# One table for the issue order of all five engines in a two-sublayer transformer step

## The chip, the cores and the metric

The kernel runs on one core of one Trainium2 chip. The metric is the device time of one execution in microseconds, as the median of several runs. The core has five engines that each issue their own instructions in a fixed sequence: TensorE (PE, with its weight loads as PEld), VectorE (DVE), ScalarE (ACT), GpSimd (POOL) and SyncE (SP), which issues most of the transfers (DMAs). An instruction waits on semaphores for what it needs from the other engines, and everything behind it on the same engine waits with it. So the same instructions in another order on an engine compute the same, and may end at another time.

## The reference

One encoder layer runs over 1024 prompt frames and over 64 sample frames, the latter with 512 cached rows. All of it is fp32.

```python
def in_proj(x, w_in, b_f):            # 1024 -> 3072 + 6 columns
    z = jnp.einsum('btd,de->bte', x, w_in)
    q_f, k_f, v_f, f_lg, u_g, v_g, q_s, k_s, v_s = jnp.split(z, _split_points(), axis=-1)
...
# FoX: softmax(q k / 8 + c_t - c_s) v, causal, c = cumsum(log_sigmoid(f))      6 heads x 64
# SB:  a = exp(log_sigmoid(z) + sum of log_sigmoid(-z) behind), a v, causal    6 heads x 64
# SGU: gelu(u) * (tril(W_s) LN(gelu(v)) + b), chunks of 128                    4 groups x 64
o = concat(o_fox, o_sgu, o_sb)
mix = (o * rsqrt(mean(o * o over a head) + RMS_EPS) * g_mix) @ w_out
x = layer_norm(ALPHA * x + mix, ln1_g, ln1_b)
x = layer_norm(ALPHA * x + square(relu(x @ w_up)) @ w_down, ln2_g, ln2_b)     # D_FF = 4096
```

The outputs are the two `x` and the new rows of keys, values, log forget gates and normalised gate values.

## The kernel before

Every fp32 operand of a large product is split into a high part (rounded to `fp32r`, by ACT) and the residue (by DVE or POOL, `lo_sub`, L98), and a product is three passes: high by high, high by low, low by high (`PASSES`). The MLP's products go by a scheme of seven block products in place of eight, with sums of weight blocks and of x blocks made beforehand.

The stages, by the times of the profile:

- **0 to about 560 us: projections and attention.** Chunks of x are loaded (`xr`, L312), transposed on PE (`xtp`, L321) and split into `xT`. Weights come as `raw` (L337) and are split (L338). Heads come in pairs: `kvfox`/`kvsb` (L362), `qfox`/`qsb` (L503), scores `Sfox`/`Ssb` (L561), softmax on ACT (`Tfox`, L536) or stick-breaking by ACT, a scan on DVE (`snsb`, L545) and a product on POOL (`sgsb`, L547). The probabilities are transposed into a PSUM tile `pt` (L609), split by ACT and DVE into `pth` (`split_pt`, L577 and L98), and multiplied with the values into `osb`/`ofox` (L619 to L622); the result is copied by ACT (`osbsb`/`osbfox`, L632) and transposed back (`otpsb`, L640). Gate projections `sgu` and `sgv` (L362) with their gelu (L758 to L761; `g1u4` and `g1u5` are those of chunks 4 and 5) and the gate's norm (L832 to L838) run beside it. `sgsb2s` and `snsb2s` belong to the sample frames.
- **The W_out steps** (`scale_wo`, L967 to L987) run beside the attention: sixteen times, a block of `w_out` is loaded into `rwo` (one buffer), scaled by `g_mix` and split into `swo` (one buffer) by ACT (L981) and DVE (L982), and stored to `wo_dr` in DRAM by two transfers (L985).
- **560 to 660 us: output projection** (`mx`, L251), with the heads' norm ahead of it (`sq`, L192, statistics `ss`, and `oTb`, L209).
- **660 to 730 us: the first layer norm**, x blocks `xo`, and the first up products.
- **730 to about 1040 us: the up product.** `Chain(p, s)` (product at L1294) makes the seven products of 256 columns `p` for a group `s` of rows, into four PSUM banks `zA` to `zD`. A bank is released by its reader: `sn` on ACT (L1305) for `zA`, sums on DVE (L1308, L1310) for others. `wr` are loaded weights (L1485), `wa` their splits (L1232), `ws` those of the sums (L1514).
- **About 1045 to 1385 us: the down product** (`Down`, L1756) from hidden rows that went through DRAM, with accumulators `acc` on DVE (L1721, L1723); then the last norms up to 1396 us.

What sets the order: the code is written as generators that are advanced in turn; the framework's scheduler then orders each engine's instructions by a simulated timeline and the dependencies. Some places take that freedom away: `in_order` gives each instruction that is traced inside it a dependency without a semaphore on the one traced before it on the same engine. `behind` does so with everything traced so far ahead of it. They stand around the W_out steps in the main loop (L1135), the first up chains (L1536, L1587, L1612 for PE alone, L1629), the last up chains (L1932) and the tail (L1999).

Of the kernel before, what the change touches and what calls it, by code (L numbers as in the profile page):

```python
# [2 lines left out]

# [1 line left out]

# [15 lines left out]
P = 128  # L21
PASSES = ((0, 0), (0, 1), (1, 0))
D = 1024
# [26 lines left out]
def build(tc, a):  # L50
    nc = tc.nc
    es = ExitStack()
    with es:
        _build(nc, tc, a, es)


def _build(nc, tc, a, es):
# [39 lines left out]
    def lo_sub(eng, out, src, hi):  # L97
        eng.tensor_tensor(out, src, hi.bitcast(F32), op=ALU.subtract)  # L98

    @contextmanager  # L100
    def in_order(prev=None, only=None):

        traced = nc.cur_bb.bb.instructions
        last = traced[-1]
        yield
        at = next(k for k in reversed(range(len(traced))) if traced[k] is last) + 1
        prev = {} if prev is None else prev
        for i in traced[at:]:
            if only is not None and i.engine != only:
                continue  # L110
# [179 lines left out]
    with ExitStack() as p1:  # L290
# [792 lines left out]
        F, A = fill(), attn()  # L1083
# [10 lines left out]
        while f_live or a_live:  # L1094
# [11 lines left out]
            if go_a:  # L1106
# [5 lines left out]
                try:  # L1112
                    c = next(A)
# [232 lines left out]
    for i in range(MIXED, NT):  # L1346
        t = ORD[i]
# [132 lines left out]
    with p3:  # L1480
# [148 lines left out]
        with in_order(border):  # L1629
# [20 lines left out]
            h4 = lp.tile([P, 2, 2, 2, 4, P], F32R, name="h4a", tag="ws")  # L1650
# [53 lines left out]
    with ExitStack() as p3:  # L1704
# [271 lines left out]
        c = NC - 1  # L1976
# [21 lines left out]
        g = 2 * c  # L1998
# [135 lines left out]
```

## Time and profile before

| | |
|---|---|
| median of 3 runs | 1400.99 us (1399.53 to 1404.98) |
| span of the profiled execution | 1396.1 us |
| median less span | 4.9 us |
| TensorE busy, idle in the span | 1324.3 us, 71.8 us |
| mean granted TensorE clock | 0.983 |
| HBM traffic over the span | 127 GB/s |

The profiled execution's time as a whole is not listed on its own; the span reaches from its first to its last instruction, and the median of the runs stands for the time around it. The page below cuts the span into 40 slices of 34.9 us; a digit is the busy share in tenths, and PEclk the clock that was granted to TensorE.

```profile
PE   7999999999988998999989999999998999999996
DVE  3576766676888288679866877777668677767677
ACT  4366665566656376334523322222256676667675
POOL 3222231245666355666422212212156765565557
PEclk9999999999999999999999999999999999999998
```

TensorE is near full in every slice but the first and the last; the other engines have free time in nearly all.

### The profile page before, as it was taken

Reading aid. Unit: us, or ns where it says so; the run is one execution under the profiler, and the core shown is the slowest. Engines: PE = TensorE matmul, PEld = TensorE weight load, DVE = VectorE, ACT = ScalarE, POOL = GpSimd, SP = SyncE. Lnnn points to the kernel's source line nnn. Section 1 sums busy time; section 2 is a strip of 40 time slices with the busy share of each in tenths; the row PEclk is TensorE's granted clock in tenths of the full one; section 3 lists DMA queues with packets and bytes.
Section 4 is the critical chain, followed back from the end, with each engine's and each line's share of the span. In section 5 each row is a group of like instructions: output and inputs, shape, how many; then the busy total and the mean of one; then the engine's idle time right before and its main releaser. Section 6 shows DMA issues by size and latency. Waiting matters only on the chain.

```text
span 1396.1 us, 24310 instructions
## 1 busy us (share of the span) xinstructions
PE 1324.3 (95%) x8827; PEld 1207.8 (87%) x8827; DVE 997.1 (71%) x1795; ACT 721.2 (52%) x1561; POOL 614.1 (44%) x667
## 2 busy tenths in 40 slices
PE   7999999999988998999989999999998999999996
PEld 7899989989987998778889999999986788887775
DVE  3576766676888288679866877777668677767677
ACT  4366665566656376334523322222256676667675
POOL 3222231245666355666422212212156765565557
PEclk9999999999999999999999999999999999999998
DMA  7355454231312346623234344443468344444343
GB/s 220 78 147 171 143 166 137 68 93 39 84 34 51 80 136 232 192 100 101 77 99 156 118 149 136 140 156 121 164 224 308 97 164 140 137 146 154 100 136 128
DMA packets 159088, 185.64 MB, mean 133 GB/s; under 512 B 27756, under 2 KB 117164, under 8 KB 158968
## 3 DMA queue, kind: packets, MB, share of 16 engines
q1 hardware_dynamic: 158968, 184.08, 41.8%
q8 instruction: 70, 1.15, 0.4%
q14 instruction: 50, 0.41, 0.1%
HBM read 117.65 MB, written 60.10 MB: 127 GB/s over the span
## 4 chain that ended last, share of the span: by engine, by line
PE 70%; DVE 10%; DMA 6%; ACT 5%; POOL 4%; issue 4%; SPq 1%; DVEq 0%; ACTq 0%; POOLq 0%
PE A L1756 9%; PE zA L1294 9%; PE zD L1294 6%; PE kvsb L362 5%; PE D L1756 5%; PE mx L251 5%; PE kvfox L362 4%; PE zB L1294 3%; PE zC L1294 3%; PE B L1756 2%; PE Sfox L561 2%; PE qfox L503 1%; PE qsb L503 1%; PE ptfox L609 1%; POOL wd L98 1%
## 5 line engine op out<-in xcount | busy, mean ns | idle before, releaser
L98 POOL TENSOR_TENSOR wa<-wr,wa 128x512 fp32r<-128x512 f32 x42 | 64.7, 1568 | 226.3 <-ACT wa L1232 226.3
L98 POOL TENSOR_TENSOR wd<-rd,wd 128x512 fp32r<-128x512 f32 x77 | 100.6, 1318 | 108.0 <-ACT wd L1232 99.3
L251 PE MATMUL mx<-xT,oTb 128*128 128x512 f32 (+1 forms) x416 | 105.2, 404 | 1.5 <-DVE oTb L98 1.5
L1294 PE MATMUL zA<-xo,ws 128*128 128x288 f32 (+1 forms) x720 | 98.4, 291 | 4.4 <-ACT sn L1305 4.4
L1294 PE MATMUL zD<-xo,ws 128*128 128x288 f32 (+1 forms) x720 | 98.0, 290 | 3.7 <-DVE h4a L1458 2.4
L1294 PEld LDWEIGHTS zA<-xo,ws 128*128 128x128 f32 x720 | 94.5, 191 | 4.6 <-ACT sn L1305 4.6
L1294 PEld LDWEIGHTS zD<-xo,ws 128*128 128x128 f32 x720 | 93.9, 189 | 4.4 <-DVE h4a L1458 2.6
L362 PE MATMUL kvfox<-wkvfox,xT 128*128 128x256 f32 (+3 forms) x624 | 93.4, 299 | 1.3 <-ACT wkvfox L338 0.5
L251 PEld LDWEIGHTS mx<-xT,oTb 128*128 128x128 f32 (+1 forms) x416 | 76.0, 188 | 20.6 <-DVE oTb L98 2.4
L1426 POOL TENSOR_TENSOR rd<-rd 128x512 f32<-128x512 f32 x56 | 79.6, 1421 | 29.6 <-DVE b L98 27.3
L547 POOL TENSOR_TENSOR sgsb<-sgsb,snsb 128x127 f32<-128x127 f32 (+7 forms) x48 | 58.5, 1219 | 75.0 <-DVE snsb L545 69.8
L362 PE MATMUL kvsb<-wkvsb,xT 128*128 128x256 f32 (+1 forms) x624 | 89.1, 288 | 0.0
L1232 ACT ACTIVATE wd<-rd 128x512 fp32r<-128x512 f32 x105 | 63.6, 623 | 45.7 <-POOL rd L1426 22.4
L362 PEld LDWEIGHTS kvfox<-wkvfox,xT 128*128 128x128 f32 (+1 forms) x624 | 84.1, 198 | 3.0 <-ACT wkvfox L338 0.9
L1756 PE MATMUL A<-wd,wd 128*128 128x512 f32 x312 | 83.3, 396 | 3.1 <-DVE acc L1723 2.2
L545 DVE TENSOR_TENSOR_SCAN snsb<-snsb,one 128x128 f32<-128x128 f32 (+7 forms) x48 | 72.5, 1513 | 14.9 <-ACT snsb L544 14.3
L362 PEld LDWEIGHTS kvsb<-wkvsb,xT 128*128 128x128 f32 (+1 forms) x624 | 80.1, 189 | 0.2
L1305 ACT ACTIVATE sn<-zA 128x256 f32<-128x256 f32 (+1 forms) x80 | 31.0, 390 | 90.6 <-PE zA L1294 80.0
L1756 PEld LDWEIGHTS A<-wd,wd 128*128 128x128 f32 x312 | 58.1, 188 | 19.2 <-DVE acc L1723 3.5
L1756 PE MATMUL A<-wd,h4a 128*128 128x512 f32 x240 | 64.2, 393 | 0.8 <-ACT h4a L1453 0.5
L1514 ACT ACTIVATE ws<-wr 128x1024 fp32r<-128x1024 f32 x28 | 29.2, 1057 | 56.8 <-DVE wr L1244 56.8
L1756 PEld LDWEIGHTS A<-wd,h4a 128*128 128x128 f32 x240 | 44.8, 188 | 11.9 <-ACT h4a L1453 0.9
(548 smaller groups left out, 3748.3 us busy)
## 6 DMA issues: line engine op xcount, KB each, us to landing
h_dr<-hh SPq DMA_DIRECT2D x30, 512.0 KB, 3.2
rd<-w_down SPq DMA_DIRECT2D x30, 512.0 KB, 4.4
wr<-w_up SPq DMA_DIRECT2D x13, 1024.0 KB, 5.4
hr<-h_dr SPq DMA_DIRECT2D x31, 384.0 KB, 3.8
h_dr<-hh SPq DMA_DIRECT2D x30, 384.0 KB, 3.2
raw<-w_in SPq DMA_DIRECT2D x44, 256.0 KB, 3.2
wo_dr<-swo SPq DMA_DIRECT2D x32, 256.0 KB, 2.6
xT<-wo_dr SPq DMA_DIRECT2D x8, 1024.0 KB, 7.5
```

Source lines behind the costliest of these rows:

```text
L98: eng.tensor_tensor(out, src, hi.bitcast(F32), op=ALU.subtract)
L251: nc.tensor.matmul(acc[0:m], oT[:, k, hx, 0:m], wo[k // 4][hw][:, k % 4, cs], start=(i == 0), stop=(i == len(seq) - 1))
L362: nc.tensor.matmul(acc[0:n, c0:c0 + n1 - n0], xT[k // 4][:, k % 4, c:c + n], wt[:, k, hw, n0:n1], start=(i == 0), stop=(i == len(seq) - 1))
L503: nc.tensor.matmul(acc[:, 0:w], wq[:, k, hw, :], xT[k // 4][:, k % 4, c:c + w], start=(i == 0), stop=(i == len(seq) - 1))
L545: nc.vector.tensor_tensor_scan(g[:, 0:n][:, ::-1], g[:, 0:n][:, ::-1], one.broadcast_to([P, n]), 1.0, op0=ALU.mult, op1=ALU.bypass)
L547: nc.gpsimd.tensor_tensor(s[:, 0:n - 1], s[:, 0:n - 1], g[:, 1:n], op=ALU.mult)
L1232: nc.scalar.activation(hi, raw, AF.Copy)
L1294: nc.tensor.matmul(z, w[:, hw, k], xop(s, bo, hx)[:, k, :], start=(new and k == 0 and j == 0), stop=(k == 3 and j == 2), skip_group_check= ...
L1305: nc.scalar.activation(c, z, AF.Copy)
L1426: eng.tensor_tensor(r[:, o], r[:, x], r[:, y], op=ALU.subtract)
L1514: nc.scalar.activation(ws[:, 0, q, c], src[:, q], AF.Copy)
L1756: nc.tensor.matmul(z, h[:, hx, q, o], wset[self.c % 2][q][:, hw, wb], start=((n in (0, 3) or n == 1 and self.c == 0) and q == 0 and j == 0 ...
```

## The change

After the program has been traced, `set_orders` goes over all instructions once. For each of the five engines it takes the instructions in the order of tracing, reads a permutation of them from the table `ORDERS` (packed as differences of 16 bits), and gives each instruction a dependency without a semaphore on the one that the table puts ahead of it. That fixes the whole sequence of every engine. `in_order` and `behind` now do nothing. No instruction is added, removed or changed. The line numbers from L100 on are higher by 6.

```diff
@@ -52,6 +54,26 @@
     es = ExitStack()
     with es:
         _build(nc, tc, a, es)
+    set_orders(tc)
+
+
+def unpack(text, kind):
+    return _np.frombuffer(zlib.decompress(base64.b85decode("".join(text.split()))), kind).astype(_np.int64)
+
+
+def set_orders(tc):
+
+    queues = {name: [] for name in ORDERS}
+    for i in tc.nc.cur_bb.bb.instructions:
+        name = str(i.engine).split(".")[-1]
+        if name in queues and i.opcode not in ("RegisterMove", "TilePoolBoundary"):
+            queues[name].append(i)
+    free = mybir.DependencyInfo(mybir.DependencyClass.NoSync, mybir.DependencyReason.DATA)
+    for name, queue in queues.items():
+        place = _np.cumsum(unpack(ORDERS[name], _np.int16) + 1) - 1
+        assert sorted(place) == list(range(len(queue))), name
+        for p, q in zip(place, place[1:]):
+            tc.add_manual_dep(queue[q], queue[p].name, free, reason="order")
@@ -97,26 +119,10 @@
-    @contextmanager
     def in_order(prev=None, only=None):
...
-            p = prev.get(i.engine)
-            if p is not None:
-                tc.add_manual_dep(i, p.name, mybir.DependencyInfo(
-                    mybir.DependencyClass.NoSync, mybir.DependencyReason.DATA), reason="in_order")
-            prev[i.engine] = i
-
-    def behind():
-
-        return in_order({i.engine: i for i in nc.cur_bb.bb.instructions})
+        return nullcontext()
+
+    behind = in_order
@@ -2110,6 +2116,100 @@
+ORDERS = {
+    "PE": r"""
...
+    "DVE": r"""
...
+    "Activation": r"""
...
+    "Pool": r"""
...
+    "SP": r"""
...
+}
```

The orders before and now agree over long stretches. Of the matmuls about a third stand at another place relative to their neighbours, of the instructions of the other engines between a third (POOL) and two thirds. Three places show what moves. A row gives the line, the operation, and the tiles written and read; the numbers behind a tile's name tell the copies apart.

**ACT at the start of the up product (715 to 730 us before).** `sn1_0` and `sn1_1` read the bank `zA` of the chains of `p` = 1 for the two groups of rows, `wa2` and `ws2` are splits of the weights of `p` = 2, which the load of `wr2` brings. Before:

```order
L1305 ACTIVATE sn1_0_9152<-zA1_0_9154 128x288 x2
L1305 ACTIVATE hh1_0_9153<-zA1_0_9154 128x288
L1232 ACTIVATE wa2_9236<-wr2_9149 128x512 x3
L1305 ACTIVATE sn1_1_9256<-zA1_1_9258 128x256 x3
L1514 ACTIVATE ws2_9338<-wr2_9149 128x1024 x2
```

Now:

```order
L1311 ACTIVATE sn1_0_9152<-zA1_0_9154 128x288
L1311 ACTIVATE sn1_1_9256<-zA1_1_9258 128x256
L1311 ACTIVATE sn1_0_9152<-zA1_0_9154 128x288
L1238 ACTIVATE wa2_9236<-wr2_9149 128x512 x2
L1311 ACTIVATE hh1_0_9153<-zA1_0_9154 128x288
L1238 ACTIVATE wa2_9236<-wr2_9149 128x512
L1311 ACTIVATE sn1_1_9256<-zA1_1_9258 128x256 x2
```

One `sn1_1` has moved from behind the three `wa2` to ahead of them; `hh1_0` has moved behind two of them. On PE the first products of both groups of `p` = 1 now come ahead of the second ones, and the first `wa2` matmul follows after eleven products and a part in place of fourteen.

**ACT near the end of the attention (549 to 560 us before).** `osbsb2_3_0` is the copy of the last but one SB head's result, and `pthsb2_3_1_0` to `_2` are the splits for the last. Before:

```order
L577 ACTIVATE pthsb2_3_0_3_7605<-ptsb2_3_0_3_7601 128x384
L543 ACTIVATE sgsb2s_7654<-Ss0sb2_7639 128x512
L544 ACTIVATE snsb2s_7655<-Ss0sb2_7639 128x512
L543 ACTIVATE sgsb2s_7654<-Ss1sb2_7640 128x64
L544 ACTIVATE snsb2s_7655<-Ss1sb2_7640 128x64
L760 ACTIVATE g1u4_7540<-g1u4_7540 128x256
L192 ACTIVATE sq0_7555<-oo0_0_7552 128x512
L758 ACTIVATE g1u5_7618<-up4_7151 128x256
L632 ACTIVATE osbsb2_3_0_7628<-osb2_3_0_7414 128x256
L577 ACTIVATE pthsb2_3_1_0_7689<-ptsb2_3_1_0_7684 128x512
```

Now:

```order
L583 ACTIVATE pthsb2_3_0_3_7605<-ptsb2_3_0_3_7601 128x384
L549 ACTIVATE sgsb2s_7654<-Ss1sb2_7640 128x64
L198 ACTIVATE sq0_7555<-oo0_0_7552 128x512
L764 ACTIVATE g1u4_7540<-up4_7151 128x256
L198 ACTIVATE sq0_7555<-oo0_1_7553 128x512
L766 ACTIVATE g1u4_7540<-g1u4_7540 128x256
L638 ACTIVATE osbsb2_3_0_7628<-osb2_3_0_7414 128x256
L583 ACTIVATE pthsb2_3_1_0_7689<-ptsb2_3_1_0_7684 128x512
L583 ACTIVATE pthsb2_3_1_1_7702<-ptsb2_3_1_1_7697 128x512
L198 ACTIVATE sq1_7575<-oo1_0_7572 128x512
L549 ACTIVATE sgsb2s_7654<-Ss0sb2_7639 128x512
```

Three of the four sample pieces and `g1u5` have moved behind `osbsb2_3_0`; a second `sq0` and the first half of `g1u4` have come ahead of it.

**SP and ACT at the start (the first 70 us before).** The load of the first block of `w_out` into `rwo0_0`, with the gain `gmx` ahead of it, on SP. Before:

```order
L444 DMA c_dr_79<-cum0_675 6x1024
L1021 DMA cbfox2_0_782<-c_dr_79 128x1024
L1021 DMA cbfox2_1_784<-c_dr_79 128x1024
L970 DMA gmx_88<-g_mix 128x8x1
L974 DMA rwo0_0_803<-w_out 128x512
L472 DMA p_fox_k<-kvsfox1_1_821 128x128
```

Now:

```order
L318 DMA xr6_257<-x_prompt 128x1024
L791 DMA bs_5419<-b_s 128x4x1
L976 DMA gmx_88<-g_mix 128x8x1
L980 DMA rwo0_0_803<-w_out 128x512
L318 DMA xr7_314<-x_prompt 128x1024
L420 DMA cl_1030<-cache_fox_logf 128x4x6
```

The load has moved from SP's place 61 to place 23, ahead of the loads `xr7` and `xr8` of x. The scaling `swo0_0` on ACT moves with it, from place 66 to place 21 (behind a copy into `xT`, ahead of a split of `kpfox`), and the last one, `swo7_1`, from place 272 to 148.

More of the change, by code (lines that the diff above doesn't have):

```diff
@@ L1 @@
+import base64
 import math
-from contextlib import ExitStack, contextmanager, nullcontext
+import zlib
+from contextlib import ExitStack, nullcontext
 import numpy as _np
@@ L98, in lo_sub @@
         eng.tensor_tensor(out, src, hi.bitcast(F32), op=ALU.subtract)
-    @contextmanager
     def in_order(prev=None, only=None):
[L103 to L110, printed above, removed]
-            p = prev.get(i.engine)
-            if p is not None:
-                tc.add_manual_dep(i, p.name, mybir.DependencyInfo(
-                    mybir.DependencyClass.NoSync, mybir.DependencyReason.DATA), reason="in_order")
-            prev[i.engine] = i
-    def behind():
-        return in_order({i.engine: i for i in nc.cur_bb.bb.instructions})
+        return nullcontext()
+    behind = in_order
     def dma_r(out, in_):
@@ new lines @@
+z)Z&~NI|GRxYAP|M<4{4?=-<3;HCeCIkZ?K~`z^`MeyBydzf)lAy#34pez%eR1r#s3WV<){RkJm(>VVv6eLoE)IcW7Z-e;#(vzgZn%ZgCdPW?BfmfjED
+{OJW)cPA8^wfrvs+zwO{7qDCS^%JuEb>zkOQLg91<KD=sH_e-cSiW8I<SZm}A7juu(Va3!Hn#A4L-_Y6<<&hPT4c-`+1T~f6z<&yN;2=XYFB`-!((uLz
+99SkWuPzdCXZoxKIj!q(6kos_3)aX8m>KHY>u`Cck}Xa{{1FFnY;MsK~ViH35-1xmRi@-`Li#Q>#1NPQy05cet%2q%6&#EMyK#<GWPKR`v#V-V}sdFUc
+SUwVJ-j9@!GG+S=_6ib}Z>3SS@?G1FzTet8whFvTiKLso(L^^=u-Jw1R(@8GihPX!xfby$jQ3&{$VW^xz7Ki;Vru;NbxCL`4Kao`%HM4Mwy{to=WL_EF
+^MD3vLJ9wna764uq2U0K5WxXG#!Z}K^EEzoxj|J-N%kG%xX1<fKBW1K9B_R|TnGK({64L9-n%Pj7WH&?G&+VeW(;+wQHt@m58y^yPUva}JXcjm6^aQXc
@@ new lines @@
+`kUe(sW0H4)o~W}U?Q(qPAf)GP{{Q)!W>14IWUeAV`Y*>4r|1
+""",
+    "DVE": r"""
+c-qxh$!;7~6umXKd+^W>4hhqO1xx;b4}edA6%va`hz$Z3ED#bxuqF~qb}0XV_yj%yBoYF#jqPstR9(~M+;d;GjgSyqDspwb_wGEL`;tnn!Y9RFB$Z}(u
+QinzzX|qg?7SgA=t>W`Ug-$ud-#4!9+CHL`CenJ8=Xj}3w>9<3o`8~_+IOMImK>*uXp4}U26%6_bEx_LZ|o>$sm1*b*Z1oS6bkAAFKEA9mxb=6@EK4yE
+Zz2h5j7Md-8>L;B2&oC9$+PU1$#496TfZt{|-;g?)GWp?pJ6GkG8nwSm7icyn?2CC(qxhX?X4WL27AZ-CQ}<TL)Ru(K!k<q4?2luz|aUz6W;OD)%+7=i
+a|`4}<|7}r=H<NF?dpFnS=FUsfg0W?m*br-vx{;7B5H???``U34Z(-U~HkJB^ISw7}irL?euj-NpNI(>Mmwr&v14E&MI@HHUa8Z-^8N@Wagvm?Pj+t0A
@@ new lines @@
+jdp`kMC6duc!^${Ju#_5?S}@WUi<0xmcxGH@lw=dm=XK4yNvn3R>e1R!!seq_OfP>gSku>;VdM%s1y{G_3up3B%wN0zEjgdd-Q*gJ&A(Lqc9sNhbI!=c
+?q1^ejeS}(3pW{yr%i?^c;3N_EpO|V8LJtSVZND`QoU|Ey|F*1wFxoKXHG_Gz5SNQHTcHN*BbgQcbCC~Uj780r=ffH#A4z2oUn>YM)evI*nlHtjhd}?4
+{lja!rQdn`s5$jZ~rr>0xEhmd(=*;$!A+f1QurIW*&H_`~}Lgq3Z
+""",
+    "Activation": r"""
+c-pO2%Z}qz5G}u*IPG+jZqy7ziywf^Nb?7Xk3b+a3nadP4MIqK01{%s2E>8|-+*AlmaiCKm{w1BI`4<=q&Ri%b<!GU2afF6<$LRKs_K+Qa#?FGfvi+`q
+`03!65>C?-HFti$UE}8F0~JdKt9({I=Fu<zjD{R@(U!9#MHIc_vB~F6P#PV>B*g*$|LzrcX-}u1HEglp!t3I5t0w(C+HVw4P>KcBbHO_zSAf2jdrBbfU
@@ new lines @@
+tos8Q{Fpmi^siIZm2@bF$>j>cGDRdm%t{Gcv|ZjU^nf4LncuI6-o7#5pw&{}rd%922{WOi^om&!*5<<CKD(y(FHNses==;(5y1T=HwfX`f)t7<@JMoF(
++cB7F#yM%>}PQ!?hXonNg@!*-=zzMHA#!aRMZyF>T3*c#*R!NhxLvZ%@fwnv+7oMv-JY-4e=>S)uLX{(Okww!7&V{0sb$1f@C0E>2lGk+;g!^pVm47eG
+yU8(!paq}?q-9Lwgi0o%yL_=0o2gscBo9GJoXXI{IDG}#D`yG}0uUi*Ed;9|@8@5s
+""",
+    "Pool": r"""
+c-oazVOGN+3=UA*&AC0_e)`7~cmwb50X&3y0H;pf?8+7s5@7AxALczu2qF3M1qxt*C7>hCz=L@_8MQ&2*YJisI;?1Y!n9Y!!V%fm>bi!O)}Az;SzOOwG
+8s6a%sb?$SGrr#_(qvIpS#GH&hM~j0JDrn<Zx#DMTzAn;&`ecU`_fShjB#ME_=1cOLM{uiq~Y8II0`PDRmvu5{4G*h}Oe>J}L7P_A_(DL#|=3x%)L$z<
@@ new lines @@
+ufzUx(aRr+oNWQ$VS0ru|*OXN=ilV%taVgrQ--SL7|)g2or#YGu!=z2Y6bphV{S1W#c+V7gZTbK+y3nX}~S^<D%z<0*H*a;pr~acq=Z0}XuO61FIq)?|
+5)(XR>DGV&wbawd~|1u=(Li}-F)tmi0K@I&`<LEln+V#f9OE^lQh!}rqf@09=4ZeMO_Y;Y_lYc{T|B5tTwvC6)S{Z99!^rXDxqxLZQv}j{Lr~Lx4)zFu
+{<X`dMcvVKiSb25n$M!bYF&;17y)hB5^W7ommA(Ws($PN(l@W&
+""",
+    "SP": r"""
+c-pN~OKX!+5Iy<wYSY*zAypco3-Ph23zZa#SX8J`UAk~1{xY}jL<GTwXni3fJ_{m<3ZhcQ8kHs{HqYakxnDHhbmfJ6XTF)ab7$t94*(JvU7K9MbM8bLu
+X#}4&v*ncnNO4me30c88%$upNWPMyGH7$1-x=~8LJ~c`&{q{tIbc<`C;D2DeCYC#&It2(%y~uhm8Xg|uCbzX5%=XiCjSj)U~zdgc--r{BhRv8fEn3uv%
@@ L2113 @@
+(
+""",
+}
 _INS = ["x_prompt", "x_sample", "cache_fox_k", "cache_fox_v", "cache_fox_logf", "cache_sb_k", "cache_sb_v",
```

54 lines of the change are left out of this document (added).

## The prediction

> **What bounds the kernel now.** I read the page first, then the stretches of the span by stage, then TensorE's waits, and last the timelines at the largest waits.
>
> ```profile
> span 1396.1 us, 24310 instructions
> PE 1324.3 (95%) x8827; PEld 1207.8 (87%) x8827; DVE 997.1 (71%) x1795; ACT 721.2 (52%) x1561; POOL 614.1 (44%) x667
> ```
>
> TensorE is busy for 1324.3 of 1396.1 us. The change removes no matmul, so an order can win only two things: the 71.8 us in which TensorE stands idle, and matmuls that run slowly. The table of stretches says where both are. Its columns are from:to in us, the length, the busy time of PE, PEld, DVE, ACT and POOL with counts, the granted TensorE clock, and DMA.
>
> ```profile
> 0.00:100.00 100.00, 86.70 (x632) 82.38 (x633) 54.50 (x137) 44.11 (x112) 26.86 (x59) 0.95 0.53 147
> 100.00:300.00 200.00, 192.04 (x1562) 186.31 (x1561) 131.72 (x353) 123.43 (x299) 50.76 (x98) 0.99 0.47 134
> 300.00:560.00 260.00, 238.67 (x1883) 230.15 (x1882) 189.45 (x315) 154.67 (x394) 147.81 (x184) 0.97 0.33 94
> 560.00:660.00 100.00, 98.15 (x480) 77.91 (x480) 80.50 (x144) 39.15 (x68) 64.62 (x65) 0.97 0.40 131
> 660.00:730.00 70.00, 62.54 (x411) 57.53 (x410) 55.04 (x86) 27.89 (x51) 27.14 (x25) 0.98 0.25 83
> 730.00:980.00 250.00, 250.00 (x1988) 250.00 (x1987) 184.68 (x274) 71.80 (x133) 56.03 (x36) 1.00 0.43 142
> ```
>
> From 730 to 980 us (the up product) TensorE has no idle time and the full clock: nothing is to be had there, whatever the order. Of the idle time, 13.3 us lie in the first 100 us, 8.0 up to 300, 21.3 up to 560 (the second half of the attention) and 7.5 between 660 and 730. The clock term of the same rows is the length times one minus the clock: 5 + 2 + 7.8 + 3 + 1.4, 19 us up to 730 us. The waits of TensorE name who ends that idle time (total, times, longest, in us):
>
> ```profile
> PE xtp L321 <- DMA xr<-x_prompt: 7.1, 2, 4.4
> PE osb L621 <- DVE pthsb L98: 6.2, 9, 1.7
> PE otpsb L640 <- ACT osbsb L632: 5.3, 4, 1.7
> PE ofox L619 <- ACT pthfox L577: 4.5, 5, 1.6
> PE zA L1294 <- ACT sn L1305: 4.4, 1, 4.4
> ...
> PE A L1756 <- DVE acc L1723: 2.5, 4, 1.0
> PE zD L1294 <- DVE h4a L1458: 2.4, 1, 2.4
> PE ofox L619 <- ACT osbfox L632: 2.0, 2, 1.8
> PE sgv L362 <- DVE sgvv L761: 1.9, 1, 1.9
> PE A L1756 <- DVE acc L1721: 1.7, 2, 1.0
> ...
> PE mx L251 <- DVE oTb L98: 1.5, 2, 0.9
> PE zD L1294 <- DVE hh L1308: 1.4, 2, 0.7
> ```
>
> No wait is a bottleneck of its own: there are many of one or two us, and nearly all end on ACT or DVE, which are far from full (52% and 71%). That is a question of order.
>
> **The change part by part.** It adds and removes no work; each engine gets another fixed order. I go through the waits above and ask what now stands ahead of the instruction that ends them.
>
> *The z bank at 726.5 us.*
>
> ```profile
> 720.52 1.57 PE L1294 MATMUL zB<-xo,wa 128*128 128x256 f32 x12
> 726.50 2.93 PE L1294 MATMUL zA<-xo,ws 128*128 128x256 f32 x12 [4.40 <-ACT sn L1305]
> ```
>
> ```profile
> 723.97 1.15 ACT L1232 ACTIVATE wa<-wr 128x512 fp32r<-128x512 f32 x2 [8.34 <-DMA wr<-w_up]
> ...
> 726.08 0.36 ACT L1305 ACTIVATE sn<-zA 128x256 f32<-128x256 f32 x1
> ```
>
> The product that waits could have its bank at once: `sn1_1` takes 0.36 us, and its input was complete before 722.1 us. But it stands behind the three `wa2` splits, and these wait 8.34 us for a weight load. In the new order the first `sn1_1` stands ahead of them, so the 4.40 us go. What is late next is `wa2` itself: TensorE now comes to it after eleven products and a part instead of fourteen. I leave 0.4 us for that: **4.0 us** won.
>
> *Attention chains.* In the rows above `osb`, `otpsb` and `ofox` wait for the split or the copy that feeds them: 6.2 + 5.3 + 4.5 + 2.0 = 18.0 us. One such place:
>
> ```profile
> 555.28 0.44 PE L640 MATMUL otpsb<-ident,osbsb 128*128 128x128 f32 x2 [1.41 <-ACT osbsb L632]
> 556.95 0.38 PE L621 MATMUL osb<-pthsb,vpsb 128*128 128x256 f32 x1 [0.68 <-DVE pthsb L98]
> ```
>
> ```profile
> 554.54 0.42 ACT L758 ACTIVATE g1u<-up 128x256 f32<-128x256 f32 x1 [1.53 <-POOL sguu L761]
> 554.86 0.37 ACT L632 ACTIVATE osbsb<-osb 128x256 f32<-128x256 f32 x1
> ```
>
> `osbsb` (and the `pthsb` behind it) stands behind a `g1u5` that waits 1.53 us for POOL; the new order has that `g1u5` seven rows behind `osbsb`, and three of the four pieces of `sgsb2s` and `snsb2s` behind it too. At most of the larger waits of this kind I find such a move, at some (309, 230 and 387 us) none. Bounds: 0 and 18.0; I take half, **9.0 us**, as the engine that is let through first only moves the next instruction's wait closer.
>
> *SGU bank.* `sgv` waits 1.9 us for `L761` on DVE, behind the norm of the chunk before it; the norm now stands behind `L761`: **1.9 us**. *Smaller ones:* `oTb` for `mx` (1.5) loses its statistics from ahead of it, I take 1.0; the accumulators of the first Down group (2.5 + 1.7) change in order but still share DVE, a third, 1.4; `h4a` and `hh` ahead of `zD` (2.4 + 1.4), half, 1.9. *The first loads:* `xtp` waits 7.1 us for landings; SP's first places change little, of these I take 1.5 (bounds 0 and 7.1). Together these are 5.8.
>
> *The W_out steps.* All sixteen (load `rwo`, scale on ACT, residue on DVE, two stores) move from 69–247 us to beside instructions that ran at 19–134 us. On SP they are moved past `xr7` and `xr8`, the last loads of x; on ACT `swo0_0` now stands ahead of copies of `xT` and splits of `kpfox`, which feed the first projections. Here is what one costs today where it is late:
>
> ```profile
> 68.85 5.34 DMA rwo<-w_out
> ```
>
> ```profile
> 74.28 0.72 ACT L981 ACTIVATE swo<-rwo,gmx 128x512 fp32r<-128x512 f32 x1 [1.22 <-DMA rwo<-w_out]
> ```
>
> ```profile
> 75.83 0.38 PE L619 MATMUL ofox<-pthfox,vpfox 128*128 128x256 f32 x1 [1.34 <-ACT pthfox L577]
> ```
>
> ```profile
> DMA to landing us min/median/max: 3.0/3.7/5.3
> ```
>
> ACT stands 1.22 us for the landing, and TensorE 1.34 us behind it. One buffer holds `rwo`, so a step takes at least a landing, the scaling and about as much again on DVE: 3.7 + 0.72 + 0.72 = 5.1 us, sixteen of them 82 us, in some 115 us. That leaves 33 us, 2.1 us to a step. From below: the 1.34 us go and nothing comes. From above: every step blocks ACT by 2 us more, 32 us. I take zero, near the lower end, because the steps fit; the waits on `ofox` are counted above already.
>
> *Slow matmuls.* Behind waits the clock drops:
>
> ```profile
> 555.00:560.00 5.00, 2.74 (x15) 2.10 (x16) 4.94 (x11) 3.55 (x8) 4.53 (x6) 0.90 0.84 242
> 560.00:565.00 5.00, 4.65 (x18) 3.89 (x18) 4.49 (x10) 2.13 (x4) 3.84 (x4) 0.50 1.02 389
> 724.00:730.00 6.00, 3.50 (x17) 3.50 (x18) 3.45 (x4) 2.40 (x5) 4.85 (x3) 0.72 0.14 34
> ```
>
> After 2.3 us of idle time within 5 us the next 5 us run at 0.50. Without the ramp, 14 us of the clock term lie between 100 and 730 us; if a third of the waits there goes, so does about a third of it: **4 us**. [...]
>
> *New waits.* At three places fewer matmuls stand between the release and the matmul that needs it (a `kvfox` bank near 29 us, `osb` near 366, the start of Down near 1050). At the size of one wait in the rows above (about 1.3 us) they cost **4 us**; bounds 0 and the whole gain.
>
> **Sum:** 4.0 + 9.0 + 1.9 + 4.3 (`mx`, Down, `zD`) + 1.5 + 4 − 4 = 20.7, 21 us. The profiled span is 1396.1 us and the median of the runs 1400.99, so 4.9 us lie around the span; an order leaves those. 1401 − 21 = **1380 us**.
>
> **Rivals.** *The waits come back.* A fixed order fits the durations that it was found with, and these move with what runs beside them:
>
> ```profile
> 401.16 0.43 DVE L837 TENSOR_TENSOR sgvv<-sgvv,gvb 128x256 f32<-128x256 f32 x1
> ...
> 405.87 1.65 DVE L837 TENSOR_TENSOR sgvv<-sgvv,gvb 128x256 f32<-128x256 f32 x1
> ```
>
> ```profile
> 405.64 1.59 POOL L547 TENSOR_TENSOR sgsb<-sgsb,snsb 128x767 f32<-128x767 f32 x1
> ```
>
> The same DVE operation takes 0.43 us, and 1.65 us while a POOL operation of 1.59 us runs. With DVE and POOL in another order other operations meet, and 1.2 us each time is as long as the waits that are to go. Then the terms that hang on ACT's and DVE's timing (9.0 + 1.9 + 4.3) and most of the clock return, and what stays is the z bank, the loads and 1 us of clock, less the new waits: 4.0 + 1.5 + 1 − 4 = 2.5, with one or two places that hold 4: **1397 us** (1391 to 1404). For it: half of the busy time of these stages is on DVE. Against it: at 726 and 555 us the blocker waits for a load or for POOL, which no such stretch brings back. [...]
>
> *Slower: the W_out steps block ACT.* ACT issues in order; a `swo` whose load is late holds the `xT` copies behind it, and in the first 100 us TensorE has little else to do (13.3 us idle already). It decides from the point where a landing passes 3.7 + 2.1 = 5.8 us, against a largest one of 5.3 us today, with DMA engines at 0.53 in that stretch. Its price is 16 × 2 = 32 us against the 21 won: **1412 us**.
>
> *Much more is won.* All of the 18.0 us of the chains, 4 us more on Down and `zD`, 5 us more of the loads and as much clock as was idle: 21 + 9 + 4 + 5 + 10 = 49, **1352 us**. Against it: the places without a move.
>
> *It does nothing* (the orders are much the same, and what moves was not late): 1401. The moved rows at 726 and 555 us speak against it.
>
> **How the numbers follow.** The forecast (a third to a half of the waits, 1366 to 1392) has 0.52, the waits that come back 0.20, the blocked ACT 0.12, the larger gain 0.13, nothing 0.03. 0.5% is 7 us, about what a measurement can tell from no change, so 1394 to 1408 counts as the same. The forecast and the larger gain are faster; of the waits that come back 0.05 are too, 0.15 the same. Faster 0.70, same 0.18, slower 0.12. The range leaves out the slow case and half of the large gain: 1357 to 1402.
>
> **What would show it.** Right: no wait over 1 us before `zA`'s second product near 726 us; `osb`, `otpsb` and `ofox` together at about 9 us of waits; a granted clock of 0.98 to 0.99 in the attention; the up product unchanged at no idle time; PE's busy time some 5 us less. The W_out steps show in who waited for `rwo`:
>
> ```profile
>   ACT swo L981: 14.8, 8
> ```
>
> Over 30 us in this row, with waits of TensorE on `xT` or `kpfox`, would prove the slow case. Wrong: waits as long as before with other names, or longer DVE operations in the attention.

## The result, and the profile after

The changed kernel is faster: 1388.08 us as the median of 16 runs (1385.87 to 1390.78), against 1397.34 us for the old kernel in 16 runs (1391.74 to 1404.98) beside them. The ratio is 0.9934, with a 95% interval of 0.9920 to 0.9949. That is 9 us, or 0.7%, where 21 us were forecast; 1388 lies in the range of 1357 to 1402.

The page of the changed kernel begins so:

```profile
span 1384.4 us, 24306 instructions
PE 1317.4 (95%) x8827; PEld 1197.6 (87%) x8827; DVE 980.4 (71%) x1795; ACT 728.0 (53%) x1561; POOL 606.4 (44%) x667
```

The profiled span is 11.7 us shorter. TensorE's busy time fell by 6.9 us (its mean granted clock rose from 0.983 to 0.994) and its idle time by only 4.8 us, from 71.8 to 67.0. The table of stretches, with the same columns as before, shows why the idle time moved so little:

```profile
0.00:100.00 100.00, 83.77 (x623) 78.86 (x624) 58.35 (x142) 48.48 (x117) 26.01 (x57) 0.98 0.71 201
100.00:300.00 200.00, 186.48 (x1496) 178.98 (x1495) 119.77 (x328) 114.86 (x273) 47.05 (x92) 0.99 0.36 103
300.00:560.00 260.00, 246.67 (x1977) 236.22 (x1976) 185.70 (x339) 163.18 (x418) 144.87 (x190) 1.00 0.35 101
560.00:660.00 100.00, 99.41 (x494) 78.69 (x493) 78.56 (x145) 40.49 (x71) 71.68 (x71) 1.00 0.37 124
660.00:730.00 70.00, 66.70 (x482) 62.81 (x481) 55.65 (x90) 27.69 (x50) 21.97 (x20) 1.00 0.31 100
730.00:980.00 250.00, 248.93 (x1971) 248.48 (x1970) 183.80 (x274) 73.42 (x134) 54.12 (x38) 1.00 0.43 146
```

Behind 300 us the waits went: 13.3 us idle in place of 21.3 up to 560, 3.3 in place of 7.5 between 660 and 730, and the clock rose from 0.97 and 0.98 to 1.00. By the length times one minus the clock, the 12.2 us that these rows had before (7.8 + 3 + 1.4) are gone. But in the first 300 us there is more idle time than before, 29.7 us in place of 21.3, and in the stretch from 100 to 300 us TensorE starts 1496 matmuls in place of 1562.

The waits of TensorE agree (total, times, longest, in us):

```profile
PE xtp L327 <- DMA xr<-x_prompt: 7.0, 3, 4.2
PE ofox L625 <- ACT pthfox L583: 5.5, 5, 2.3
PE Sfox L567 <- DVE mfox L539: 4.1, 6, 1.3
...
PE D L1762 <- DVE acc L1727: 2.8, 1, 2.8
PE osb L627 <- DVE pthsb L120: 2.1, 4, 0.7
...
PE otpsb L646 <- ACT osbsb L638: 1.2, 2, 1.0
...
PE ofox L625 <- ACT osbfox L638: 0.8, 1, 0.8
```

One row of before belongs beside them:

```profile
PE Sfox L561 <- DVE mfox L533: 0.8, 2, 0.6
```

`osb` behind `pthsb` is down from 6.2 to 2.1 us, `otpsb` from 5.3 to 1.2, and the wait for `sn` at the z bank is gone. Of the first head pairs, `ofox` behind `pthfox` is up from 4.5 to 5.5, and `Sfox` behind `mfox` is up from 0.8 to 4.1.

Stretches of equal time do not hold equal work, so for what follows the two traces were laid over each other by work. Each matmul counts as the usual interval of its form in the old trace, and the **lag** is the time at which a kernel has done the same amount of TensorE work, less the time in the old profile. Positive is late, in us:

| old time | 50 | 100 | 150 | 200 | 300 | 400 | 500 | 600 | 700 | 730 | 980 | 1050 | 1080 | 1380 |
|---|---|---|---|---|---|---|---|---|---|---|---|---|---|---|
| changed kernel | -0.6 | 1.0 | 8.8 | 12.6 | 10.3 | 5.0 | 0.6 | -8.7 | -6.1 | -13.3 | -12.2 | -8.8 | -13.3 | -13.0 |

The lag compares one execution with one other. Four kernels below have the old order up to 255 us, and their lags are -3.3 to 0.6 us at 200 us and -5.5 to 0.5 us at 250, so a difference of a few us between two profiles can be chance. Gains at the end are also larger by the lag than by the medians: 13.0 against 9.3 us here.

The new order loses 12 us between 100 and 200 us, wins 21 between 200 and 600, and 7 at the z bank near 726 us. So the question is not where a gain got lost: it is there, and something at the front costs half of it.

### The profile page after: what moved, and what is told of

Its sections match the earlier page's. It is cut to its first block, busy times and chain, and to the rows that moved or that the text cites. A ratio compares the mean times of both kernels' runs of the same rounds, so it can differ in the third digit from the quotient of the medians.

```text
span 1384.4 us, 24306 instructions
## 1 busy us (share of the span) xinstructions
PE 1317.4 (95%) x8827; PEld 1197.6 (87%) x8827; DVE 980.4 (71%) x1795; ACT 728.0 (53%) x1561; POOL 606.4 (44%) x667
## 4 chain that ended last, share of the span: by engine, by line
PE 53%; DVE 11%; DMA 5%; ACT 4%; POOL 4%; issue 3%; SPq 0%; POOLq 0%; DVEq 0%; ACTq 0%
PE A L1762 9%; PE zA L1300 8%; PE mx L257 7%; PE zD L1300 5%; PE D L1762 5%; PE kvsb L368 3%; PE zB L1300 3%; PE zC L1300 3%; PE B L1762 2%; DMA h_dr<-hh 1%; PE sgv L368 1%; DVE snsb L551 1%; DMA raw<-w_in 1%; PE sgu L368 1%; PE ds L1808 1%
## 5 line engine op out<-in xcount | busy, mean ns | idle before, releaser
L120 POOL TENSOR_TENSOR wa<-wr,wa 128x512 fp32r<-128x512 f32 x42 | 60.2, 1462 | 231.9 <-ACT wa L1238 231.9
L120 POOL TENSOR_TENSOR wd<-rd,wd 128x512 fp32r<-128x512 f32 x77 | 105.1, 1379 | 105.8 <-ACT wd L1238 78.3
L1432 POOL TENSOR_TENSOR rd<-rd 128x512 f32<-128x512 f32 x56 | 76.6, 1368 | 11.5 <-DVE b L120 8.9
L551 DVE TENSOR_TENSOR_SCAN snsb<-snsb,one 128x128 f32<-128x128 f32 (+7 forms) x48 | 68.0, 1422 | 13.9 <-ACT snsb L550 12.6
L1729 DVE TENSOR_TENSOR acc<-acc,A 128x512 f32<-128x512 f32 x73 | 49.6, 682 | 30.7 <-PE A L1762 30.7
L120 DVE TENSOR_TENSOR pthfox<-ptfox,pthfox 128x512 fp32r<-128x512 f32 (+1 forms) x60 | 37.6, 635 | 31.9 <-ACT pthfox L583 31.5
```

The source lines that it names most:

```text
L551: nc.vector.tensor_tensor_scan(g[:, 0:n][:, ::-1], g[:, 0:n][:, ::-1], one.broadcast_to([P, n]), 1.0, op0=ALU.mult, op1=ALU.bypass)
L1432: eng.tensor_tensor(r[:, o], r[:, x], r[:, y], op=ALU.subtract)
L1729: nc.vector.tensor_tensor(out, out if other is None else other, bank, op=ALU.add)
```

## The experiments

All kernels hold the same instructions as the two above. Since the table takes any order, they are orders put together from the old and the new one. The tables also show where the change lies: only 8% of the matmuls follow another matmul than before (the third given in the description counts matmuls at another place in the queue), but 34% to 59% of the instructions of the other engines follow another one. The ratios are to the old kernel, run beside each on the same chip.

### Is the loss at the front the price of the gain?

Two kernels change the order at one point in time: on each engine all that started before it in one profile comes first, in that profile's order, and the rest follows in the other's.

```diff
 before255_after:  order = old[started before 255 us in the old profile]     + new[rest]
 after265_before:  order = new[started before 265 us in the changed profile] + old[rest]
```

> On each engine the old order for all that started in the first 255 us of the old profile (with all W_out steps), and then the new order for the rest. Theory A and B: the loss of 10 to 12 us in the first part goes, the gain after it stays: ratio 0.985. Theory C (the later gain is bought with the early loss): 0.993 or higher.

> The new order for all that started in the first 265 us of the changed kernel's profile (the same amount of TensorE work as 255 us of the old one), and the old order for the rest. Theory A and B: the early loss stays, the gain is gone: 1.007. Theory C: 1.000 or below, the ACT and DVE time that was freed is used by the old order too.

Measured: `before255_after` 0.9860 (0.9837 to 0.9883), 1376.63 us, faster than both kernels; `after265_before` 1.0109 (1.0082 to 1.0136). The lags:

| old time | 200 | 300 | 500 | 600 | 730 | 980 | 1380 |
|---|---|---|---|---|---|---|---|
| before255_after | -1.1 | 0.5 | -10.6 | -20.1 | -23.6 | -22.8 | -23.9 |
| after265_before | 14.3 | 11.8 | 11.8 | 11.8 | 11.8 | 11.8 | 17.8 |

Up to 980 us the loss and the gain simply add: -22.8 + 11.8 = -11.0, against -12.2 for the changed kernel. With the old front the new order wins 23.9 us by the lag and 18.6 by the medians. With the new front the old order stays 12 us late up to 980 us; the 6 us more at 1380, with which the medians are 15.2 us apart and the ratio is above the 1.007 expected, were not traced. Theory C falls here.

### Is it the W_out steps?

`wo_only` is the old order with the W_out steps alone at their new places; `wo_back` the new order with these steps alone at their old places.

```diff
 wo_only:  old order, 81 instructions (gmx, 16 loads, 16 on ACT, 16 on DVE, 32 stores)
-  beside work of  69 to 247 us
+  beside work of  19 to 140 us
 wo_back:  new order, the same 81 instructions
-  beside work of  19 to 140 us
+  beside work of  69 to 247 us
```

> The old orders, with the W_out steps alone put where the change has them (beside work of 19 to 140 us). Theory A: the old kernel loses 8 to 12 us between 100 and 200 us, ratio 1.007. Theory B: within 2 us of before, ratio 1.000. Theory C: it loses between 100 and 200 us and wins it back after 200 us, ratio 0.998 to 1.002.

> The new orders, with the 81 instructions of the W_out steps (load, scaling on ACT, residue on DVE, stores) put back beside the work beside which they ran in the profile of before (about 69 to 247 us); everything else in the new order. At the same amount of TensorE work the changed kernel is 12.7 us behind the old one at 200 us, and 12 to 13 us ahead from 730 us on. Theory A (the early W_out steps hold ACT and with it TensorE between 100 and 200 us): the loss goes, the lag at 200 us falls to under 4 us, and the time is 8 to 11 us below the changed kernel: ratio to before 0.986. Theory B (other moves of the first 300 us cost it): within 2 us of the changed kernel, ratio 0.993. Theory C (the early steps pay for the gain later, since ACT and DVE are free of them after 150 us): the lag at 200 us falls, and the gain between 300 and 600 us falls with it: ratio 0.993 or higher.

Measured: `wo_only` 1.0122 (1.0098 to 1.0147), so the move by itself costs 17 us, more than the 8 to 12 of theory A, and its lag is 17.4 us at 200 us. But `wo_back` gave 0.9929 (0.9908 to 0.9950), no better than the changed kernel. Its lag is 6.7 us at 200 us and back at 11.9 us at 275, where the changed kernel has 12.2: what was saved at the front is lost between 200 and 275 us. The largest wait there is one of `ofox` for `osbfox` on ACT, 2.8 us in place of 0.8; what makes it was not traced. The time is that of theory B, but none of the three theories has this course.

To see the front without the steps, they were put far behind it, in the new order and in the old one; `rwo` and `swo` have buffers of their own for it, since a later tile uses theirs.

```diff
 wo_late, old_wo_late: the new and the old order with the 81 instructions beside work of 270 to 470 us
-  name=f"rwo{k}_{half}", tag="sq", bufs=1      name=f"swo{k}_{half}", tag="wst", bufs=1
+  name=f"rwo{k}_{half}", tag="rwo", bufs=1     name=f"swo{k}_{half}", tag="swo", bufs=1
```

> The new orders with the W_out steps put beside work that ran at 270 to 470 us in the profile of before; rwo and swo get buffers of their own for that. Theory A (in the new order the W_out steps are what costs the first 265 us): the lag behind before at 200 us of old time falls from 12.6 to under 3 us; Theory B (the other moves of that stretch cost as much): it stays at 6 us or more (with the steps put back it was 6.7). Time: A 0.984 to 0.987 if the second half of the attention carries the steps for nothing, B 0.989; 0.993 or more if the steps cost there what they cost early.

> The old orders with the W_out steps beside work of 270 to 470 us, with buffers of their own as in wo_late. It shows what the old order pays for them at 69 to 247 us. If they lie there almost free (two waits, 1.3 and 2.0 us): the lag at 255 us is -2 to -4 us. If they cost what they cost early in the new order: -8 to -11 us. Time: in the second half of the attention they then cost something again, ratio 0.997 to 1.006.

Measured: `wo_late` 0.9955 (0.9934 to 0.9975), `old_wo_late` 1.0061 (1.0044 to 1.0078). By the lag of `wo_late` theory A holds (1.5 us at 200 us); by its time the steps cost later about what they cost early.

| old time | 100 | 200 | 300 | 400 | 500 | 600 |
|---|---|---|---|---|---|---|
| wo_late | -5.2 | 1.5 | -1.2 | 1.3 | 0.2 | -9.2 |
| old_wo_late | -2.6 | -3.9 | -6.1 | 0.7 | 4.6 | 3.4 |

Now the front can be taken apart at 200 us. In the new order the steps cost 12.6 - 1.5 = 11.1 us there, in the old order at their old places 3.9 us. Without them the new front is 1.5 - (-3.9) = 5.4 us slower than the old. So of the 12.6 us, 11.1 - 3.9 = 7.2 are the steps' place and 5.4 the other moves. The old order, however, has steps up to 247 us. At 255 us, where both orders have done them all, the lags are 10.1 (changed kernel), -1.0 and -6.1, and the same sums give 11.1 and 6.1 us for the steps, 5.0 for their place and 5.1 for the other moves. That the steps cost the new front 11 us is well clear of chance; the shares of 5 to 7 and of 5 us are hardly larger than the spread given above. The second half of the attention does not carry the steps for nothing either: the old order loses 9.5 us there (-6.1 to 3.4), and the new one wins 8.0 us between 300 and 600 us in place of the 20.6 of `before255_after`.

### What makes early steps dear?

The prediction had weighed one wait, ACT's for the landing of `rwo`. In the changed kernel it can be seen just where the loss is, first ACT, then DVE, then TensorE, in the timelines:

```profile
113.36 0.72 ACT L987 ACTIVATE swo<-rwo,gmx 128x512 fp32r<-128x512 f32 x1 [3.13 <-DMA rwo<-w_out]
```

```profile
114.12 0.75 DVE L988 SCALAR_TENSOR_TENSOR swo<-rwo,gmx,swo 128x512 fp32r<-128x512 f32 x1 [3.84 <-ACT swo L987]
...
120.95 0.75 DVE L988 SCALAR_TENSOR_TENSOR swo<-rwo,gmx,swo 128x512 fp32r<-128x512 f32 x1 [1.94 <-ACT swo L987]
```

```profile
116.50 0.39 PE L567 MATMUL Sfox<-kpfox,qdfox 128*128 128x256 f32 x1 [1.32 <-DVE mfox L539]
...
124.99 0.38 PE L625 MATMUL ofox<-pthfox,vpfox 128*128 128x256 f32 x1 [2.26 <-ACT pthfox L583]
```

ACT waits for a landing; DVE, in order, waits for ACT; and the maximum `mfox` that releases a bank for `Sfox` stands behind that on DVE. The wait at 124.99 us comes from the next step: behind its residue at 120.95 stand the next `mfox` on DVE (122.39 us) and then `Tfox` and `pthfox` on ACT (123.18 and 124.45 us). `wo_only` shows two more links, in the timelines of ACT and TensorE:

```profile
37.16 0.38 ACT L469 ACTIVATE kvsfox<-kvfox 128x256 f32<-128x256 f32 x1 [6.36 <-DMA p_fox_v<-kvsfox]
...
134.08 0.72 ACT L987 ACTIVATE swo<-rwo,gmx 128x512 fp32r<-128x512 f32 x1 [5.02 <-DMA wo_dr<-swo]
```

```profile
37.59 0.48 PE L492 MATMUL pkfox<-ident,kvsfox 128*128 128x128 f32 x1 [2.70 <-ACT kvsfox L469]
...
136.50 1.54 PE L615 MATMUL ptfox<-ident,Tfox 128*128 128x128 f32 x6 [5.09 <-ACT Tfox L542]
```

and in SP's waits from 10 to 160 us:

```profile
SPq L991 <- ACT swo L987: 17.9, 11, 5.4
```

SP holds the stores of `swo` for ACT for 17.9 us, and the stores of `p_fox_v` stand behind them; `kvsfox` on ACT waits 6.36 us for such a store, since it needs its buffer (the store was issued at 32.10 us, behind one of `swo`, and took 5 us to land); and the next `swo` waits 5.02 us for the landing of the last one's store. Two kernels loosen this, one link after the other.

```diff
 wo_only_2buf: as wo_only, each load of rwo one step earlier on SP
-  name=f"rwo{k}_{half}", tag="sq", bufs=1
+  name=f"rwo{k}_{half}", tag="rwo", bufs=2
 wo_only_free: as wo_only_2buf, each pair of stores of swo one step later on SP
-  name=f"swo{k}_{half}", tag="wst", bufs=1
+  name=f"swo{k}_{half}", tag="swo", bufs=2
```

> As wo_only (old orders, early W_out steps: 1.0122), but rwo has two buffers of its own, and SP issues each load one step earlier, so that it can land before ACT comes to it. Theory A1 (ACT stands for the landing of rwo, 14.5 us there, and what is behind it on ACT makes TensorE wait): ACT's wait for rwo falls under 5 us and the loss shrinks from 17 us to under 8, ratio 1.005. Theory A2 (the scaling on ACT, the residue on DVE and the transfers themselves take the time of others in the first 140 us): the loss stays, 1.010 or more, though the wait for rwo goes.

> As wo_only_2buf (1.0100), and swo has two buffers as well, with each pair of stores one step later on SP. There ACT stood 6.8 us for the landing of the stores of swo (once 4.8 us, with TensorE 4.8 us behind it), and kvsfox 6.3 us for stores of p_fox_v that stand on SP behind the stores of swo. Theory A3 (three queues in order, ACT, SP and the two single buffers, hold each other up): those waits fall under 3 us together and the loss shrinks to under 6 us, ratio 1.004 or less. Theory A2 (the work itself takes the time): 1.008 or more.

Measured: `wo_only_2buf` 1.0100 (1.0066 to 1.0134), `wo_only_free` 1.0043 (1.0029 to 1.0057). The rows by tile tell who ACT's `swo` waited for; in `wo_only`, in `wo_only_2buf` and in `wo_only_free`:

```profile
  DMA rwo<-w_out: 14.5, 6
  DMA wo_dr<-swo: 5.0, 1
```

```profile
  DMA wo_dr<-swo: 6.8, 3
  DMA rwo<-w_out: 3.1, 1
```

```profile
  DMA rwo<-w_out: 3.0, 1
...
  DMA wo_dr<-swo: 0.3, 1
```

The landing of `rwo` fell from 14.5 to 3.1 us, and the lag at 600 us only from 12.5 to 11.3: the wait that the prediction had priced was not what cost time, because the stores held ACT in its place. With the stores loosened as well the lag at 600 us is 1.9 us. The transfers by themselves are not the cause: in `wo_only_free` the DMA engines are as busy from 20 to 60 us as in `wo_only` (0.67 and 0.62), and the stores of `swo` take no less time to land (4.0 and 3.3 us in the median). The median time still shows 6 us, of which 2.3 come in the tail (3.1 at 980 us, 5.4 at 1380), and that part was not traced further. So A1 and A2 fall, and A3, which gave 1.004 or less, stands, at its edge: the early steps cost little by their work in the old order; they cost when ACT, SP and one buffer each wait for one another. The second buffer of `swo` and the later stores were changed together, so which of the two counts for more is open.

The same was done to the changed kernel:

```diff
 after_free: the new order; rwo and swo with two buffers, loads one step earlier, stores one step later
```

> The changed kernel with its own orders, but two buffers each for rwo and swo, each load of W_out one step earlier on SP and each pair of stores one step later (what took the loss from 12.5 to 2.5 us in the old order). Theory A3 (in the changed kernel too the early loss is this coupling): the lag at 200 us of old time falls from 12.6 us to 4 or less, and the time by 8 to 10 us, ratio 0.986 to 0.988. Theory B2 (with the steps taken out of the first 265 us altogether the lag was 1.5 us, but their work on ACT and DVE, 16 times 1.5 us, does not fit among the rest of the new order whatever the buffers): the lag stays at 8 us or more, ratio 0.991 to 0.994.

Measured: 0.9901 (0.9877 to 0.9926), 1384.49 us. The lag at 200 us fell from 12.6 to 8.5 us: a third of the loss, between the two theories. At 980 us it is 4.0 us ahead of the changed kernel, and at 1380 us of this profile 0.6; the interval of the ratio just reaches that of the changed kernel. A fall of 4 us is about the spread between two profiles. So in the changed kernel this coupling is likely to cost some us, which is not shown, and most of the loss stays. SP no longer shows a wait for `swo` among its largest; what is left at the front is chiefly this:

```profile
PE Sfox L567 <- DVE mfox L539: 4.7, 4, 2.7
```

That is the wait which the new order has without the steps too (3.1 us up to 215 us in `wo_late`). Which of the moves on DVE and TensorE makes it was not tried, so this part of the loss stays open.

### The gains by themselves

The z bank was tried with one instruction, on ACT, in the old order:

```diff
 L1311 ACTIVATE hh1_0_9153<-zA1_0_9154 128x288
+L1311 ACTIVATE sn1_1_9256<-zA1_1_9258 128x256
 L1238 ACTIVATE wa2_9236<-wr2_9149 128x512 x3
-L1311 ACTIVATE sn1_1_9256<-zA1_1_9258 128x256 x3
+L1311 ACTIVATE sn1_1_9256<-zA1_1_9258 128x256 x2
```

> The old orders with one instruction moved: on ACT the first sn1_1 goes ahead of the three wa2 splits (the wait of 4.40 us near 726 us). The prediction's step: the wait and the slow matmuls behind it go, 5 to 6 us, ratio 0.996. Rival: TensorE only comes sooner to the wa2 matmuls, which are late with their load, and waits there instead: ratio 0.999 to 1.000, with a new wait for wa2.

Measured: 0.9962 (0.9939 to 0.9985), 5.3 us by the ratio; the lag goes from -2.8 us at 715 us, where the order is still the old one, to -6.9 at 740, 4.1 us. TensorE's and ACT's timelines:

```profile
720.57 1.57 PE L1300 MATMUL zD<-xo,ws 128*128 128x256 f32 x12
723.81 1.69 PE L1300 MATMUL zA<-xo,ws 128*128 128x256 f32 x12 [1.67 <-ACT sn L1311]
```

```profile
717.92 0.38 ACT L1311 ACTIVATE sn<-zA 128x256 f32<-128x256 f32 x1 [5.06 <-PE zA L1300]
721.29 1.15 ACT L1238 ACTIVATE wa<-wr 128x512 fp32r<-128x512 f32 x2 [2.98 <-DMA wr<-w_up]
```

The wait of 4.40 us is gone, and with it the slow run of twelve (1.69 us against 2.93). The second `sn1_1`, still behind the splits, now makes a wait of 1.67 us. The new order, which brings other first products ahead, has neither:

```profile
711.50 1.58 PE L1300 MATMUL zC<-xo,wa 128*128 128x256 f32 x12
712.92 4.81 PE L1300 MATMUL zA<-xo,ws 128*128 128x288 f32 x36
```

The attention and the output projection were tried as one window:

```diff
 attn_only: old[started before 255 us] + new[up to the work of 640 us] + old[rest]
```

> The new order only for what starts between 255 and 640 us of the old profile (second half of the attention, output projection), the old order ahead of it and behind it. The prediction's step gave 9.0 us for the chains, 1.9 for the SGU bank, 1.0 for mx and some 3 us of clock, 15 us: ratio 0.989. From the lag of the whole change (10.3 us at 300, -8.7 at 600) it should be 19 to 20 us: 0.986. If the gain is used up by waits behind it: 0.993 or more.

Measured: 0.9915 (0.9897 to 0.9932), 11.7 us, between the values expected. The lag is -1.3 us at 250 and -21.1 at 600 us, so 20 us are won; from 650 to 730 us it goes from -19.9 to -14.7. A wait stands there that neither the old nor the new order has, first on ACT, then on TensorE:

```profile
700.25 0.41 ACT L1311 ACTIVATE sn<-zA 128x288 f32<-128x288 f32 x1 [7.55 <-DMA h_dr<-y]
```

```profile
700.72 3.25 PE L1300 MATMUL zA<-xo,ws 128*128 128x288 f32 x12 [6.44 <-ACT sn L1311]
...
713.31 1.58 PE L1300 MATMUL zA<-xo,ws 128*128 128x256 f32 x12
```

It is not the wait of 4.40 us: that one, ahead of the product of 256 columns, is gone (713.31 us), though `sn1_1` still stands behind the `wa2` splits. Here ACT stands ahead of the first `sn1_0`, which is in front of those splits, until a store of hidden rows (`h_dr`) has landed; in the old kernel the same `sn1_0` runs at 708.87 us and waits for no landing. Two orders put together can make a wait that neither has. Why `sn1_0` needs that landing in this order was not traced.

At last, `before255_after` with the old order also around the start of Down, where the changed kernel's lag rises by 3.4 us from 980 to 1050 us and falls by 4.5 up to 1080:

```diff
 mix3: old[before 255 us] + new[to 985 us] + old[to 1050 us] + new[rest]
```

> Old order for all that started before 255 us of the old profile, then the new order up to the end of the up product (985 us old time), then the old order up to 1050 us, then the new one. The changed kernel loses 3.6 us between 980 and 1050 us and wins 4.5 us just behind. If both are independent: 2 to 4 us below before255_after (0.986), ratio 0.984. If the win at 1075 us only takes back what was lost ahead of it: the same 0.986.

Measured: 0.9883 (0.9850 to 0.9916), not to be told from 0.9860. Its lag stays at -30.2 and -30.1 us at 980 and 1050 us and then falls back to -26.1 at 1150. The gain at 1075 us only takes back what was given ahead of it. (Up to 250 us, where its order is the old one, this profile happened to be 5.5 us quicker.)

## Why the prediction was half right

**Right: the place of the gain, and the waits as its mechanism.** Behind 255 us the forecast's terms were 4.0 (z bank) + 9.0 (chains) + 1.9 (SGU bank) + 4.3 (`mx`, Down, `zD`) + 4 (clock), 23 us. `before255_after` won 23.9 us by the lag and 18.6 by the medians. That the two sums meet is partly luck, since the terms do not.

The chains were sized well: their rows, 18.0 us before, are down to 2.1 + 1.2 + 5.5 + 0.8 = 9.6 us, 8.4 won of 9.0 forecast. The clock was not. 4 us were forecast on the ground that a third of the waits takes a third of the clock term with it; but TensorE's idle time between 300 and 730 us fell from 30.6 to 17.2 us, less than half, and the clock term fell from 12.2 us to nothing. That is also why `attn_only`, some 15 us by the terms, measured 20 by the lag: its clock is 1.00 from 80 to 660 us, against 0.98 in the old kernel. Between 300 and 560 us the clock is 0.97 in the old kernel, and 1.00 in the changed kernel, in `before255_after` and in `after_free`.

The z bank was 4.0, and the slow twelve behind it another 1.4 (2.93 us against 1.57, at a clock of 0.72 from 724 to 730 us); alone it measured 5.3, in the whole change 7.2. Down and `zD` brought 1 us of 3.3 (lag -22.8 at 980, -23.9 at 1380). The first loads brought nothing of 1.5: 7.1 us before, 7.0 after.

**Wrong: the W_out steps, taken at zero.** Early in the new order they cost 11.1 us, where the old order paid 3.9 (at 200 us) or 6.1 (at 255 us) at their old places, 5 to 7 us more; alone in the old order the move cost 17 us. The step that failed is the sentence "I take zero, near the lower end, because the steps fit". It set a landing and the two scalings, 5.1 us, against 7.2 us to a step, as if load, scaling and store were a chain that only had to fit on the average. The stores and their landings were left out of that chain, though the one buffer of `swo` puts them in it, and so was SP, on which they stand ahead of the stores that `kvsfox` needs. In the old order these links are shown to be the cause, by `wo_only_free`; in the changed kernel loosening them took a third of the loss, about the spread between profiles, and the rest stays open. In the changed kernel the landing took at most 4.4 us and so never came near the 5.8 us from which the rival was to decide; its rows by tile read

```profile
  DMA rwo<-w_out: 14.2, 8
...
DMA to landing us min/median/max: 2.7/4.0/4.4
```

so the rival's mechanism was half right (ACT in order, 14.2 us of waits for `rwo` in 8 times), its point of decision wrong, and its price of 32 us twice what `wo_only` measured. The sign that was set for it, more than 30 us in this row, was blind: the row had 14.8 us in 8 times before and has 14.2 in 8 now. How long ACT stands in all does not tell what stands behind it.

**Mis-sized: the new waits, 4 us.** The other moves at the front cost about 5 us. Of the three places named, the start of Down did get a wait, `D` behind `acc`, 2.8 us; the large ones at the front are at none of them but at `Sfox` behind `mfox`, from 0.8 to 4.1 us.

**The sum.** By the lag about 24 us were won and 10 (at 300 us) to 12.6 (at 200 us) lost at the front, which leaves 13 us in the profile; the medians leave 9. 21 had been forecast because a gain of the right size stood against a loss of 4. The 1401 from which the 21 us were taken was the median of three runs, and sixteen gave 1397.34. The 4.9 us "around the span" set that median against another execution; in the profiled run of the changed kernel 1386.09 us stand against a span of 1384.4.

**The rival of longer DVE operations** did not come about: DVE is busy 980.4 us in place of 997.1, POOL 606.4 in place of 614.1. The operation that had taken 1.65 us takes at most 0.43 us in all its nine places. Waits came back all the same, by order: TensorE's idle time is 67.0 us against 71.8, in part under other names.

**The clock** behaved as the rows of before had it: with fewer waits the stretch from 300 to 560 us runs at 1.00. Only the ramp that the prediction set aside in the first 100 us is none: before, the clock there was 1.00 from 16 to 57 us, 0.57 from 57 to 65 us and 0.66 from 77 to 82, behind waits of 2.7 and 1.3 us.

## What to carry to other kernels

Lay two traces over each other by work done, not by time: a total of 9 us (13 by the lag) was 24 won and 10 to 13 lost, and a kernel put together from the two orders confirmed it and was the better one (0.986). Know the spread of such a comparison from kernels that have the same order in a stretch; here it was up to 5.5 us. Where a chain of load, scaling and store is moved among other work, ask on which in-order queues its pieces stand and what is behind each of them; that it fits on the average says little. Here a second buffer for the load alone won nothing that could be measured (1.0122 and 1.0100); with one for the store too and later stores it was 1.0043. Look for a release that stands behind work which waits for a load: moving one instruction was worth 5.3 us.

## What was not expected of the hardware

The clock falls behind waits shorter than the 4.40 us of before, and not behind every wait of the same length. In the changed kernel the stretches around the wait of 2.26 us at 125 us read

```profile
120.00:125.00 5.00, 2.74 (x25) 2.53 (x23) 2.59 (x7) 3.10 (x6) 0.00 (x0) 1.00 0.56 191
125.00:130.00 5.00, 5.00 (x30) 5.00 (x31) 3.99 (x11) 3.25 (x7) 0.00 (x0) 0.66 0.33 96
```

The wait of 2.26 us is followed by 5 us at 0.66 with TensorE busy throughout, 1.7 us lost by the clock, so here it cost about 1.75 times its length. That is not a rule. The same wait at the start of Down, for the same instruction, was followed by a drop in the changed kernel and by none in `before255_after`:

```profile
1036.84 0.63 PE L1762 MATMUL D<-wd 128*128 128x512 f32 x1 [2.79 <-DVE acc L1727]
```

```profile
1037.00:1042.00 5.00, 5.00 (x16) 3.93 (x17) 2.19 (x5) 0.60 (x1) 4.86 (x7) 0.66 0.93 284
```

```profile
1026.04 0.50 PE L1762 MATMUL D<-wd 128*128 128x512 f32 x1 [2.82 <-DVE acc L1727]
```

```profile
1026.00:1031.00 5.00, 4.96 (x22) 4.07 (x23) 3.34 (x6) 0.60 (x1) 4.86 (x7) 1.00 0.86 265
```

Other waits in the timelines of the two kernels, and the clock of the stretch behind each:

| kernel | wait ended at, us | wait, us | clock | stretch, us |
|---|---|---|---|---|
| old | 233.12 | 1.81 | 1.00 | 233 to 236 |
| old | 309.25 | 1.58 | 0.50 | 309.85 to 313.26 |
| old | 1028.21 | 2.37 | 1.00 | 1028 to 1033 |
| changed | 60.23 | 3.05 | 0.50 | 61 to 64 |
| changed | 1369.00 | 2.24 | 1.00 | 1369 to 1374 |

So the length of a wait alone does not tell whether such a drop follows, and a part of what the clock gave in one execution may be chance.
